# Attention in half blocks: rows of two heads by 64 queries over 192 keys, in a two-layer decoder trunk

## The chip, the core and the metric

The kernel runs on one core of one Trainium2 chip. The time is device microseconds of one execution; for the kernel before, three runs give a median of 1915.66 us (1914.08 to 1919.38). TensorE (PE in the profile, its weight loads PEld), VectorE (DVE), ScalarE (ACT), GpSimd (POOL) and the DMA queues of SyncE (SP) work side by side and wait for each other through semaphores. PSUM, in which matmuls leave their results, is used in banks of 128 x 512 float32.

## The reference

Two layers over 1024 positions of width 1024, float32. In each layer a token mixer (attention on 512 channels beside a causal pooling mixer on the other 512) is followed by a SwiGLU network of width 2816, each between two norms and with a gate. What the change touches is the sliding-window attention: 8 query heads of 64 channels share 2 key heads (4 query heads each), blocks of 128 queries see their own block and the one before, and a query sees the last 128 positions, itself included.

```python
def sliding_window_attention_with_sinks(q, k, v, sinks):
    ...
    k_cat = jnp.concatenate([jnp.pad(kb, pad)[:, :-1], kb], axis=2)
    v_cat = jnp.concatenate([jnp.pad(vb, pad)[:, :-1], vb], axis=2)
    scores = jnp.einsum("bnqkgd,bnskd->bnkgqs", qb, k_cat).astype(jnp.float32)
    scores = scores * (HEAD_DIM ** -0.5)
    ...
    valid = (diff[None] >= 0) & (diff[None] < WINDOW) & (key_abs >= 0)
    scores = jnp.where(valid[None, :, None, None], scores, NEG_INF)
    sink = ...
    probs = jax.nn.softmax(jnp.concatenate([scores, sink], axis=-1), axis=-1)[..., :-1]
    out = jnp.einsum("bnkgqs,bnskd->bnqkgd", probs.astype(v.dtype), v_cat)
    return out.reshape(B, S, N_HEADS * HEAD_DIM)
```

## The kernel before, in words

**Number format.** A float32 value is split into a high part in float32r (a copy on ScalarE, L215) and a low part, what is left (a subtraction on VectorE, L216). A product then takes three matmuls, high by high, high by low and low by high (`mm3`, L254 to L259).

**Stages.** The 1024 positions are worked on in two halves of 512 rows, four token tiles of 128 each. Per layer and half there are projections (`q_pass`, `kv_pass`, `u_pass`), attention, pooling (`pool_mix`), the output projection (`mix_out`), norms, and the SwiGLU network in seven products of half-sized matrices for eight. Each is a generator that yields between pieces; `run` (L640) steps one dense stage and with it the side streams in proportion. The attention of the first half is such a side stream beside the projections of the second half; that of the second half is stepped beside `mix_out` of the first half, then beside `u_pass`, then beside the first products of the SwiGLU network. Two further side streams are the pooling and the sums for the adaptive norm (`ada_sum`, VectorE). A scheduler then orders each engine's instructions over all streams; every engine works through its own list in that order.

**Attention before.** A block is one token tile; a group is one block and one key head n with its four query heads. Per block:

- `att_rotary` (L731) rotates, `att_keys` (L746) splits values and keys. Keys stand as high and low in two orders, are transposed by four matmuls with a unit matrix (L774) and copied twice, as own keys of this block and as earlier keys of the next (`sa`, 256 keys).
- `att_queries` (L790) does the same for four query heads (L798), into `qT`.
- `att_scores` (L806): for each pair u of heads one PSUM bank, two heads of 128 queries by 256 keys, two matmuls each (L813, L814); VectorE adds the mask and takes the row maximum (L816).
- `att_softmax` (L823): exponentials on ScalarE (L835), scaling by the reciprocal sums, three on VectorE (L841) and one on ScalarE (L843).
- `att_probs` (L845): four transposes per pair (L851), then the split into `pth` (ScalarE) and `ph` (VectorE), 512 columns.
- `att_values` (L859): the stationary operand holds the 64 value channels of one key head beside 64 zeros (`vz`), the moving one the transposed probabilities. One three-matmul product each for the earlier and the own keys, 256 columns; everything of a block gathers in one bank `pv`, which one ScalarE copy (L879) takes out.

In `attention` (L885) the scores of a group are written before the probabilities of the group before it, and the values one pair later still. Banks named `msc` come from a ring of three that scores, transposes and the side streams share; `pv` has one bank, `acc`, for the dense stages, four.

## Time and profile before

| | |
|---|---|
| median of 3 runs | 1915.66 us |
| the profiled execution, its own time | 1912.51 us |
| its span, first to last instruction | 1910.7 us |
| granted TensorE clock, mean | 0.997 |
| TensorE busy | 1866.3 us, 98% |
| VectorE busy | 1545.1 us, 81% |
| ScalarE busy | 950.5 us, 50% |
| attention's value matmuls | 384, of 256 columns |
| attention's score matmuls | 256, of 256 columns |
| transposes of probabilities | 256, of 128 columns |

A row such as `L813 PE MATMUL msc<-sa,qT 128*128 128x256` names the line, the engine, what is written and read by the program's tile names, the weights' shape and the result's. A TensorE duration runs from a matmul's start to its modelled end; neighbours overlap, so what one matmul occupies is read from the distance between starts. "Idle before" tells how long an engine stood and for whom.

### The profile page before, as it was taken

Reading aid. Unit: us, or ns where it says so; the run is one execution under the profiler, and the core shown is the slowest. Engines: PE = TensorE matmul, PEld = TensorE weight load, DVE = VectorE, ACT = ScalarE, POOL = GpSimd, SP = SyncE. Lnnn points to the kernel's source line nnn. Section 1 sums busy time; section 2 is a strip of 40 time slices with the busy share of each in tenths; the row PEclk is TensorE's granted clock in tenths of the full one; section 3 lists DMA queues with packets and bytes.
Section 4 is the critical chain, followed back from the end, with each engine's and each line's share of the span. In section 5 each row is a group of like instructions: output and inputs, shape, how many; then the busy total and the mean of one; then the engine's idle time right before and its main releaser. Section 6 shows DMA issues by size and latency. Waiting matters only on the chain.

```text
span 1910.7 us, 26084 instructions
## 1 busy us (share of the span) xinstructions
PE 1866.3 (98%) x8978; PEld 1539.2 (81%) x8978; DVE 1545.1 (81%) x2898; ACT 950.5 (50%) x1789; POOL 26.8 (1%) x84
## 2 busy tenths in 40 slices
PE   6999999999999999999999989999999999999997
PEld 4887788888888888888888868888888887888886
DVE  5999886668898888788879998846889888877687
ACT  4876795653222223445548667845622222244452
POOL 1000000000000000000000000000000000000000
PEclk9999999999999999999999999999999999999999
DMA  9355563555655665944554464536654565574342
GB/s 324 115 155 153 163 226 122 186 177 183 204 179 189 208 207 178 323 137 145 183 168 128 133 183 165 177 110 208 215 188 150 198 209 202 197 252 150 115 152 102
DMA packets 227428, 341.86 MB, mean 179 GB/s; under 512 B 16952, under 2 KB 124360, under 8 KB 227296
## 3 DMA queue, kind: packets, MB, share of 16 engines
q1 hardware_dynamic: 227152, 340.17, 54.2%
q8 instruction: 70, 1.15, 0.2%
q14 instruction: 62, 0.51, 0.1%
q0 software_dynamic: 32, 0.00, 0.0%
q10 hardware_dynamic: 112, 0.04, 0.0%
HBM read 267.25 MB, written 72.89 MB: 178 GB/s over the span
## 4 chain that ended last, share of the span: by engine, by line
PE 79%; DVE 11%; DMA 5%; ACT 3%; issue 1%; SPq 0%; DVEq 0%; ACTq 0%
PE acc L255 24%; PE acc L258 24%; PE acc L259 24%; DMA ar<-in_ada_w_dram 2%; DVE lo L216 2%; DVE ada L289 2%; PE msc L851 1%; PE msc L519 1%; ACT hi L215 1%; DMA raw<-in_w_up_dram 1%; PE pv L255 1%; DVE ph L216 1%; DMA ar<-x 1%; DVE sb L816 1%; PE pv L258 1%
## 5 line engine op out<-in xcount | busy, mean ns | idle before, releaser
L215 ACT ACTIVATE hi<-raw 128x1024 fp32r<-128x1024 f32 (+1 forms) x388 | 332.4, 869 | 365.8 <-PE acc L258 196.2
L216 DVE TENSOR_TENSOR lo<-raw,hi 128x1024 fp32r<-128x1024 f32 (+1 forms) x388 | 380.0, 986 | 123.6 <-ACT hi L215 122.8
L255 PE MATMUL acc<-t,hi 128*128 128x512 f32 x704 | 274.6, 390 | 1.5 <-ACT hi L215 1.5
L258 PE MATMUL acc<-t,hi 128*128 128x512 f32 x704 | 274.0, 389 | 0.0
L259 PE MATMUL acc<-t,lo 128*128 128x512 f32 x704 | 271.9, 389 | 0.0
L255 PE MATMUL acc<-bh,hi 128*128 128x512 f32 x520 | 202.8, 390 | 0.0
L259 PE MATMUL acc<-bh,lo 128*128 128x512 f32 x520 | 202.4, 389 | 0.0
L255 PE MATMUL acc<-hT,hi 128*128 128x512 f32 x480 | 189.7, 395 | 0.6 <-DVE fn L638 0.6
L258 PE MATMUL acc<-hT,hi 128*128 128x512 f32 x480 | 188.4, 392 | 0.0
L259 PE MATMUL acc<-hT,lo 128*128 128x512 f32 x480 | 187.7, 392 | 0.0
L1107 DVE TENSOR_TENSOR fn<-acc,fn 128x512 f32<-128x512 f32 x220 | 150.2, 683 | 37.4 <-PE acc L259 37.4
L255 PEld LDWEIGHTS acc<-t,hi 128*128 128x128 f32 x704 | 132.2, 188 | 30.8 <-ACT hi L215 3.9
L259 PEld LDWEIGHTS acc<-t,lo 128*128 128x128 f32 x704 | 132.2, 188 | 29.0 <-DVE lo L216 1.5
L258 PEld LDWEIGHTS acc<-t,hi 128*128 128x128 f32 x704 | 132.2, 188 | 27.2
L258 PE MATMUL acc<-ph,hi 128*128 128x512 f32 x320 | 124.6, 389 | 0.0
L1043 ACT ACTIVATE fn<-fn 128x512 f32<-128x512 f32 x44 | 27.8, 633 | 180.3 <-DVE fn L1107 180.3
L289 DVE SCALAR_TENSOR_TENSOR ada<-ar,c_act,ada 128x512 f32<-128x512 f32 x140 | 104.6, 747 | 12.0 <-DMA ar<-in_ada_w_dram 11.0
L259 PEld LDWEIGHTS acc<-bh,lo 128*128 128x128 f32 x520 | 97.6, 188 | 20.4
L255 PEld LDWEIGHTS acc<-bh,hi 128*128 128x128 f32 x520 | 97.6, 188 | 20.0
L255 PEld LDWEIGHTS acc<-hT,hi 128*128 128x128 f32 x480 | 90.2, 188 | 18.9 <-DVE fn L638 1.4
L259 PEld LDWEIGHTS acc<-hT,lo 128*128 128x128 f32 x480 | 90.1, 188 | 18.2
L255 PE MATMUL acc<-hi 128*128 128x512 f32 x256 | 101.1, 400 | 2.8 <-DVE fn L638 1.6
(315 smaller groups left out, 3834.6 us busy)
## 6 DMA issues: line engine op xcount, KB each, us to landing
ar<-in_ada_w_dram SPq DMA_DIRECT2D x160, 256.0 KB
raw<-in_w_gate_dram SPq DMA_DIRECT2D x44, 512.0 KB
raw<-in_w_up_dram SPq DMA_DIRECT2D x44, 512.0 KB
raw<-in_w_in_dram SPq DMA_DIRECT2D x80, 256.0 KB
raw<-keeps SPq DMA_DIRECT2D x40, 512.0 KB
keeps<-fn SPq DMA_DIRECT2D x66, 256.0 KB
two_b<-in_w_down_dram SPq DMA_DIRECT2D x30, 512.0 KB
raw<-keepa SPq DMA_DIRECT2D x25, 512.0 KB
```

What stands on the lines that cost most here:

```text
L215: nc.scalar.activation(hi, src, AF.Copy)
L216: recent["split"] = nc.vector.tensor_sub(lo, src, hi.bitcast(F32))
L255: ins = nc.tensor.matmul(dst, lh, rh, start=first, stop=False)
L258: nc.tensor.matmul(dst, lh, rl, start=False, stop=False)
L259: return nc.tensor.matmul(dst, ll, rh, start=False, stop=last)
L289: ins = nc.vector.scalar_tensor_tensor(acc, w, c_act[:, i : i + 1], acc, op0=ALU.mult, op1=ALU.add)
L519: ins = nc.tensor.transpose(bank[:, t * P : (t + 1) * P], src[t], ident)
L816: nc.vector.tensor_tensor_reduce(out=s[:, ii, :], in0=bank[:, ii * 2 * P : (ii + 1) * 2 * P], in1=mask[:, min(blk, 1), :], scale=SCALE, sc ...
L851: nc.tensor.transpose(bank[:, i * P : (i + 1) * P], s[:, ii, ck * P : (ck + 1) * P], ident)
L1043: nc.scalar.activation(g, g, AF.Silu)
L1107: nc.vector.tensor_add(halves_of(dst)[m], bank, halves_of(src)[m])
```

## The change

Rows become half blocks. `att_queries` lays the columns of `qT` out as half (64 queries), head, query, so that a row tile of 128 is two heads by 64 queries of one half. Half h of a block sees the 192 keys from 64 h on (`SPAN`), where all 128 queries saw 256. One mask of 192 columns serves all tiles, and the first block of a layer reads only its own keys (`att_seen`).

A group is now one block and a number r: it holds both halves, half 0 with key head r and half 1 with the other (`n = h ^ r`). A score bank carries 192 + 192 columns. Its 384 columns are transposed as three chunks of 128: half 0's first 128 keys, then a middle chunk whose first 64 columns are half 0's last keys and whose other 64 are half 1's first keys, then half 1's last 128 keys. The outer chunks of both row tiles fill one bank (four transposes, 512 columns to split), the middle chunks another (two, 256 columns).

The value products are three per group for both row tiles together: earlier values of head r, own values of the other head, and for the middle chunk a tile `bd` that holds own values of one head over the first 64 rows beside earlier values of the other head over the last 64. That tile is filled per block by three ScalarE copies (`att_vals`), and `pv` is taken out by four copies over 64 partitions. The value tiles are two, used in turn, and one `bd`, in place of a ring of five; `pth` is one tile of 768 columns in place of two of 512; `qT` has two. Zeros are written once per layer and half of the attention's rooms (`att_room`). Value products of a group are written as one piece, a step before the next group's softmax; the queries of the second key head are written after the first step of a block, and the next block's rotation in the block's second group. In the first block the unseen columns are zeroed on GpSimd.

```diff
-        mix=dict(cfa=2, cfb=2, qkv=6, bqkv=1, uT=4, pt=2, vz=5, rt=1, qT=1, pth=2, pwh=1, pwl=1),
+        mix=dict(cfa=2, cfb=2, qkv=5, bqkv=1, uT=4, pt=2, vz=2, rt=1, qT=2, pth=1, bd=1, pwh=1, pwl=1),
...
+    def att_room():
+        attn["v"] = [t_("vz", [P, 2, 3, HD], F32R) for _ in range(2)]
+        attn["mix"] = t_("bd", [P, 2, 4, HD], F32R)
...
+    def att_vals(blk, qkv):
+        v, mix = attn["v"][blk % 2], attn["mix"]
+        vsrc = qkv[:, QK:QKV].rearrange("p (n d) -> p n d", d=HD)
+        nc.scalar.activation(v[:, 0, 0:3:2, :], vsrc, AF.Copy)
+        nc.vector.tensor_sub(v[:, 1, 0:3:2, :], vsrc, v[:, 0, 0:3:2, :].bitcast(F32))
+        if blk:
+            before = attn["v"][1 - blk % 2]
+            nc.scalar.activation(mix[QH:, :, 0:4:3, :], before[QH:, :, 0:3:2, :].bitcast(F32), AF.Copy)
+        for n in range(NKV):
+            nc.scalar.activation(mix[:QH, :, 2 - n, :], v[:QH, :, 2 * n, :].bitcast(F32), AF.Copy)
...
+    def att_scores(blk, r, u, qTs, mx, s):
         kT = attn["k", blk]
         bank = msc_bank()
-        for ii in range(2):
-            dst = bank[:, ii * 2 * P : (ii + 1) * 2 * P]
-            q = qT[:, (2 * u + ii) * P : (2 * u + ii + 1) * P]
-            nc.tensor.matmul(dst, q, kT[:, 2 * n, :], start=True, stop=False)
-            nc.tensor.matmul(dst, q, kT[:, 2 * n + 1, :], start=False, stop=True)
+        for h in range(2):
+            n, cs = h ^ r, att_seen(blk, h)
+            dst = bank[:, h * SPAN : (h + 1) * SPAN][:, cs]
+            q = qTs[n][:, (2 * h + u) * P : (2 * h + u + 1) * P]
+            for o in range(2):
+                keys = kT[:, 2 * n + o, h * QH : h * QH + SPAN][:, cs]
+                nc.tensor.matmul(dst, q, keys, start=o == 0, stop=o == 1)
...
+    def att_probs(blk, sts, ends, probs):
         bank = msc_bank()
+        chunks = ([0] if blk else []) + [2] if ends else [1]
+        for i in chunks:
+            for u in range(2):
+                at = (i + u) * P
+                nc.tensor.transpose(bank[:, at : at + P], sts[u][:, i * P : (i + 1) * P], ident)
+        cs = slice(chunks[0] * P, (chunks[-1] + 2) * P)
+        to = slice(0, 2 * P) if not ends else slice(chunks[0] * P, 4 * P)
+        split(*(p[:, to] for p in probs), bank[:, cs])
...
+    def att_values(blk, r, probs, pmid, cat, t):
...
+        v, before = attn["v"][blk % 2], attn["v"][1 - blk % 2]
+        at = 2 * (1 - r)
+        parts = [(before, r, probs, 0)] if blk else []
+        parts += [(v, 1 - r, probs, 2 * P), (attn["mix"], at, pmid, 0)]
+        for k, (src, c, (ph, pl), p0) in enumerate(parts):
+            vh, vl = (src[:, j, c : c + 2, :].rearrange("p a d -> p (a d)") for j in range(2))
+            opening, closing = r == 0 and k == 0, r == 1 and k == len(parts) - 1
+            ins = mm3(
+                pv[:, r * 2 * P : (r + 1) * 2 * P], vh, vl, ph[:, p0 : p0 + 2 * P], pl[:, p0 : p0 + 2 * P],
+                opening, closing, None if opening else attn["open"],
+            )
...
+            for n in range(NKV):
+                ns = slice(n * HD, (n + 1) * HD)
+                for h in range(2):
+                    g = h ^ n
+                    nc.scalar.activation(
+                        cat[ns, :, t * P + h * QH : t * P + (h + 1) * QH],
+                        pv[ns, g * 2 * P : (g + 1) * 2 * P].rearrange("p (j q) -> p j q", j=GRP), AF.Copy,
+                    )
...
+            if late:
+                att_values(*late)
+                late = None
+            if cur and r == 1:
+                att_vals(blk, qkvs[t])
```

The change also moves instructions. On TensorE, in the first layer and first half, at the fifth group (the first of the third token tile), its second pair of scores stood among the transposes of the group before it; `sb` holds the probabilities, `sa` the keys. Before:

```order
L258 MATMUL acc<-lo,hT 128x256
L851 MATMUL msc<-ident,sb 128x128
L813 MATMUL msc<-sa,qT 128x256
L851 MATMUL msc<-ident,sb 128x128 x3
L814 MATMUL msc<-sa,qT 128x256
L813 MATMUL msc<-sa,qT 128x256
L814 MATMUL msc<-sa,qT 128x256
L851 MATMUL msc<-ident,sb 128x128 x3
L255 MATMUL pv<-pth,vz 128x256
L851 MATMUL msc<-ident,sb 128x128
L259 MATMUL acc<-hi,hT 128x256
```

and now, with the new line numbers (L836 scores, L883 transposes, L260 to L264 the three-matmul product), the same group:

```order
L264 MATMUL acc<-hi,hT 128x256
L836 MATMUL msc<-sa,qT 128x192 x4
L883 MATMUL msc<-ident,sb 128x128 x4
L836 MATMUL msc<-sa,qT 128x192 x4
L883 MATMUL msc<-ident,sb 128x128 x2
L260 MATMUL acc<-hi,hT 128x256
```

Both pairs of scores and all transposes of the group before now stand in one row of runs, with no dense product between them. The value products of that earlier group follow 24 dense products later, as one piece of nine. Before, a group's value products were two pieces of six, such as this one, behind the first scores of the fifth group:

```order
L813 MATMUL msc<-sa,qT 128x256
L814 MATMUL msc<-sa,qT 128x256
L255 MATMUL pv<-pth,vz 128x256
L258 MATMUL pv<-ph,vz 128x256
L259 MATMUL pv<-pth,vz 128x256
L255 MATMUL pv<-pth,vz 128x256
L258 MATMUL pv<-ph,vz 128x256
L259 MATMUL pv<-pth,vz 128x256
L255 MATMUL acc<-hi,hT 128x256
```

Now:

```order
L264 MATMUL acc<-hi,hT 128x256
L260 MATMUL pv<-pth,vz 128x256
L263 MATMUL pv<-ph,vz 128x256
L264 MATMUL pv<-pth,vz 128x256
L260 MATMUL pv<-pth,vz 128x256
L263 MATMUL pv<-ph,vz 128x256
L264 MATMUL pv<-pth,vz 128x256
L260 MATMUL pv<-pth,bd 128x256
L263 MATMUL pv<-ph,bd 128x256
L264 MATMUL pv<-pth,bd 128x256
L260 MATMUL acc<-hi,hT 128x256
```

On ScalarE, where the third token tile of that half is taken out of `pv` and values are split, before:

```order
L832 ACTIVATE st<-st 128x4
L835 ACTIVATE sb,st<-sb,st 128x256 x4
L879 ACTIVATE cfa<-pv 128x4x128
L755 ACTIVATE vz<-qkv 128x64 x2
L843 ACTIVATE sb<-sb,st 128x256
```

and, at the same place, now (L863 exponentials, L768 values, L774 and L772 the mixed tile, L912 the way out of `pv`):

```order
L858 ACTIVATE st<-st 128x4
L863 ACTIVATE sb,st<-sb,st 128x192
L768 ACTIVATE vz<-qkv 128x2x64
L863 ACTIVATE sb,st<-sb,st 128x192
L774 ACTIVATE bd<-vz 64x2x64
L912 ACTIVATE cfa<-pv 64x4x64 x4
L772 ACTIVATE bd<-vz 64x2x2x64
L774 ACTIVATE bd<-vz 64x2x64
L863 ACTIVATE sb,st<-sb,st 128x192
L220 ACTIVATE hi<-pt 128x512
L870 ACTIVATE sb<-sb,st 128x192
```

The copies into the mixed tile and out of `pv`, which read what value products write or free, now stand among the exponentials of a group, and the last exponential stands behind them.

164 lines of the change are left out of this document (73 added, 91 removed).

## The prediction

> **What bounds the kernel now.** I read the page's busy shares first, then the busy time by stretch, then the order in time on TensorE, then the groups by shape on VectorE and ScalarE.
>
> ```profile
> span 1910.7 us, 26084 instructions
> PE 1866.3 (98%) x8978; PEld 1539.2 (81%) x8978; DVE 1545.1 (81%) x2898; ACT 950.5 (50%) x1789; POOL 26.8 (1%) x84
> ```
>
> TensorE is busy for 98% of the span, so a matmul taken away is time taken away, unless a wait grows in its place. The attention lies in two stretches, one in each layer. The rows give, after the stretch and its length, the busy us of PE, PEld, DVE, ACT and POOL, the granted clock, DMA share and GB/s.
>
> ```profile
> 60.00:260.00 200.00, 194.07 (x1136) 161.38 (x1135) 184.76 (x543) 150.67 (x374) 5.67 (x21) 1.00 0.51 156
> 1000.00:1240.00 240.00, 231.11 (x1332) 193.42 (x1331) 212.67 (x596) 181.04 (x439) 7.18 (x22) 0.99 0.50 157
> 160.00:180.00 20.00, 16.84 (x82) 12.48 (x81) 18.70 (x48) 9.72 (x20) 0.42 (x2) 1.00 0.60 169
> 180.00:200.00 20.00, 18.47 (x95) 14.27 (x95) 19.16 (x48) 13.34 (x34) 0.00 (x0) 1.00 0.69 198
> 260.00:280.00 20.00, 18.80 (x111) 15.89 (x110) 15.53 (x42) 19.70 (x47) 0.27 (x1) 1.00 0.66 209
> 1100.00:1120.00 20.00, 17.26 (x85) 13.38 (x84) 18.60 (x50) 11.85 (x27) 0.00 (x0) 1.00 0.64 182
> 1120.00:1140.00 20.00, 17.25 (x83) 12.72 (x82) 18.44 (x47) 13.29 (x35) 0.00 (x0) 0.95 0.63 183
> 1200.00:1220.00 20.00, 18.80 (x114) 16.05 (x113) 16.84 (x47) 19.71 (x46) 0.27 (x1) 1.00 0.66 214
> ```
>
> In the first stretch TensorE is idle for 6 of 200 us, in the second for 9 of 240, while VectorE is at 92% and 89%: the two are near their limits together. Where TensorE does idle, another engine is full: VectorE at 160 to 200 and 1100 to 1140 (10.2 us of idle TensorE in all), ScalarE at 260 to 280 and 1200 to 1220 (2.4 us). So the change is worth its TensorE time, if VectorE falls with it and ScalarE does not rise too far.
>
> **The change part by part.** A matmul's duration here is its latency; what it occupies is the distance between starts. Columns below: start, length, engine, line, operation, count.
>
> ```profile
> 91.12 0.28 PE L255 MATMUL pv<-pth,vz 128*128 128x256 f32 x1
> 91.24 0.28 PE L258 MATMUL pv<-ph,vz 128*128 128x256 f32 x1
> 91.36 0.28 PE L259 MATMUL pv<-pth,vz 128*128 128x256 f32 x1
> 91.48 0.39 PE L255 MATMUL acc<-hT,hi 128*128 128x512 f32 x1
> 91.71 0.40 PE L258 MATMUL acc<-hT,hi 128*128 128x512 f32 x1
> 158.35 0.93 PE L851 MATMUL msc<-ident,sb 128*128 128x128 f32 x7
> 53.67 0.81 PE L364 MATMUL msc<-ones_r,ar 128*128 128x1 f32 x6
> ...
> 166.06 0.08 PEld L387 LDWEIGHTS msc<-ph,picks 128*4 128x4 f32 x1 [0.95 <-ACT ph L215]
> 166.06 0.19 PEld L255 LDWEIGHTS acc<-hi 128*128 128x128 f32 x1
> ...
> L851 PE MATMUL msc<-ident,sb x256: 270/272/331, 84.2 to 1227.5; 128*128 128x128 f32 x128
> L364 PE MATMUL msc<-ones_r,ar x32: 164/250/266, 23.7 to 54.2; 128*128 128x1 f32 x24, 1*128 1x1 f32 x8
> ```
>
> *Values.* 256 columns occupy 0.12 us (91.12 to 91.48 over three). Per token tile 24 such matmuls become 18, and 12 in the first tile of a layer, which has no tile before it: over 16 tiles 384 become 276. 108 x 0.119 = **12.9 us**.
>
> *Transposes of the probabilities.* A run of seven lasts 0.93 us and one of them 0.27, so they start (0.93 - 0.27) / 6 = 0.11 us apart. The built program issues 184 in place of 256: 72 x 0.11 = **7.9 us**. If one occupied no more than its 128 columns at the slope of the rows above (0.23 us for 512, 0.119 for 256, thus 0.43 ns per column), it would be 0.064 and the term 4.6.
>
> The Trainium skill (TensorE: Matmul & The Clock Gate, Part 4) gives about 275 ns for a transpose in a kernel's context; the median of 272 ns agrees as a latency, but as a price it would make this term 19.8 us, and the run of seven shows that it isn't one.
>
> *Scores.* The same 256 matmuls remain, 224 of them with 192 columns for 256, and 16 each with 128 and 64. By the slope 192 columns need 0.091 us. But six matmuls of a single column start (0.81 - 0.25) / 5 = 0.112 us apart: with almost nothing to stream, something that each matmul brings along lasts 0.11. The load of 128 weight columns is 0.11 longer than that of 4 (0.19 against 0.08), so I take it to be the weight load. Every score matmul loads 128 fresh columns, so I take 0.112, not 0.091: 256 x (0.119 - 0.112) = **1.8 us**. With the slope alone it would be 224 x 0.0275 + 16 x 0.055 + 16 x 0.082 = 8.4.
>
> The Trainium skill speaks on both sides, on the same page: its section LDWEIGHTS has P/1.2 ns for P columns, 107 ns for 128, which the 0.112 bears out; its section Back-to-back issue gap has N/2.4 + 2.5 ns, 82.5 for 192 columns, and by that alone the scores would save 8 us or more.
>
> Sum on TensorE: 12.9 + 7.9 + 1.8 = **22.6 us**, 1.4 per token tile; from 17.5 (4.6 for transposes, nothing for scores) to 29.2 (scores by the slope).
>
> ```profile
> L816 DVE CUSTOM_DVE_ANT_0 sb<-msc,mask 128x256 f32<-128x256 f32 x128 | 50.4, 416 | 6.0 <-PE msc L814 5.6
> L216 DVE TENSOR_TENSOR ph<-msc,pth 128x512 fp32r<-128x512 f32 x64 | 43.7, 686 | 2.6 <-ACT pth L215 2.0
> L841 DVE TENSOR_SCALAR sb<-sb,st 128x256 f32<-128x256 f32 x96 | 28.1, 348 | 0.5
> L287 DVE TENSOR_SCALAR ada<-ar,c_act 128x512 f32<-128x512 f32 x20 | 9.6, 479 | 0.0
> L707 DVE TENSOR_TENSOR qkv<-acc,bqkv 128x512 f32<-128x512 f32 x16 | 10.6, 682 | 0.1
> L696 DVE TENSOR_TENSOR qkv<-acc,bqkv 128x256 f32<-128x256 f32 x12 | 4.4, 413 | 2.6 <-PE acc L259 2.6
> ...
> L835 ACT ACTIVATE sb<-sb,st 128x256 f32<-128x256 f32 x128 | 63.7, 506 | 6.3 <-DVE st L828 6.3
> L215 ACT ACTIVATE hi<-raw 128x512 fp32r<-128x512 f32 x167 | 102.7, 629 | 93.1 <-PE acc L258 35.3 <-PE acc L259 33.3 <-issue 18.6
> L215 ACT ACTIVATE pth<-msc 128x512 fp32r<-128x512 f32 x64 | 37.8, 597 | 22.0 <-PE msc L851 21.8
> L794 ACT ACTIVATE hi<-qkv 128x256 fp32r<-128x256 f32 x32 | 13.2, 412 | 5.7 <-PE acc L259 4.9 <-DVE ada L289 0.8
> L755 ACT ACTIVATE vz<-qkv 128x64 fp32r<-128x64 f32 x32 | 6.6, 252 | 10.9 <-DVE qkv L696 7.4 <-PE pv L259 3.5
> L879 ACT ACTIVATE cfa<-pv 128x512 f32<-128x512 f32 x8 | 4.7, 587 | 0.3 <-PE pv L259 0.3
> L392 ACT ACTIVATE ar<-msc 4x512 f32<-4x512 f32 x2 | 1.2, 588 | 2.0 <-PE msc L388 2.0
> ```
>
> *VectorE.* Two-operand work falls by 1.05 ns per column (682 for 512, 413 for 256), scaling by 0.51 (479, 348). Masks: 53.2 us to 112 x 0.349 + 8 x 0.28 + 8 x 0.215 = 43.0. Probability splits: 64 of 0.686 become 28 of it and 36 of 0.413, 9.7 us less. Scaling: 33.4 to 29.6. Value splits: 32 of 0.23 become 16 of 0.30, 2.7 less. In all 26 us less, 1.6 per tile. TensorE loses 1.4, so neither takes the other's place as the limit.
>
> *ScalarE.* Its slope is 0.85 ns per column (629 for 512, 412 for 256). Exponentials lose 8.2 us, the fourth scaling 2, probability copies 7.8 (28 of 0.597, 36 of 0.38), value copies 3.2. The way out of pv becomes four copies over 64 partitions for one over 128; 4 partitions cost what 128 do (588 against 587), so each of 256 columns costs 0.41: 64 x 0.41 - 16 x 0.587 = 16.8 more. The mixed values are new: 14 of 0.41 and 32 of 0.305, 15.5 more. Together **+11 us**, 0.7 per tile. ScalarE is idle for 49 of the first 200 us, which hides it, but not at 260 to 280 and 1200 to 1220, where it is full: about one tile's 0.7 in each, **+1.5 us** with what queues behind it.
>
> *Waits.* The work between scores and second transposes now stands closer (the order shows four runs, 4 scores, 4 transposes, 4 scores, 2 transposes, back to back in about 12 of 32 groups). All take a bank of a ring of three, so the fourth run needs the first's bank, once VectorE's two mask reductions have read it: 2 x (0.35 + 0.08) = 0.86 us, and half of an instruction in hand, 0.34. TensorE covers 4 x 0.11 + 4 x 0.112 = 0.9 meanwhile. The difference, 0.3 to 0.4 us in 12 groups, is **+5 us**; it could be nothing, since before also has such runs, or 1.2 us each with two splits of 0.69 queued ahead (14). Against it, the 10.2 us that TensorE idles beside a full VectorE hold about three tiles; 3 x 1.6 = **-4.8 us**. Queries of both key heads at a tile's start, the zeroing on GpSimd in a layer's first tile and the four small sink copies have dense products behind them and count as nothing; uncovered, one query chain (0.41 for the high parts, as much for the low, four transposes of 0.11, 0.60 for the copy) is 1.9 us, in 16 tiles 30.
>
> Sum: -22.6 + 1.5 + 5 - 4.8 = **-21 us**. The profiled execution, 1912.5 us, would become 1891.5. It lies 3.2 below the median of the runs, 1915.7; from that I predict **1895 us**, the forecast's own range 1888 to 1902.
>
> **The rivals.**
>
> *Scores shrink with their columns* (for: the slope of the rows; against: the single-column run). 6.6 us more: 1888.
>
> *The fourth run waits longer* (for: VectorE at 92%, so splits queue ahead of the masks; against: the products between runs in the other 20 groups). 14 in place of 5, and VectorE's relief spent in it: -21 + 9 + 4.8 = -7: 1908, or 1903 with the relief kept.
>
> *ScalarE becomes what is waited for*, and the kernel slower. One mixed-value tile, two value tiles and one tile of high probability parts are now reused: the value copies of a token tile must wait until the last value products of the one before have ended, and the exponentials stand behind them in ScalarE's queue. The row of such a wait before:
>
> ```profile
> ACT vz L755 <- PE pv L259: 1.7, 1, 1.7
> ```
>
> At 1.7 us and 0.7 of added work in every tile, 16 x 2.4 = 38 us against 22.6: +16, 1931. It decides from 1.4 us per tile on the path. For it speaks the order on ScalarE, where the copies stand ahead of the tile's last exponential; against it the quarter of ScalarE's time that is idle, and the 24 products of TensorE after the value products, which do not wait for these exponentials.
>
> *The change removes no work on TensorE* is excluded by the counts of the built program (184, 276, narrower scores).
>
> **How the numbers follow.** Forecast 0.60; narrow scores 0.12; longer fourth run 0.18; ScalarE 0.10. What this kernel's measurement tells from no change is about 0.3%, 5.7 us: faster is below 1910, slower above 1921. The first two are faster throughout, of the third 0.13, of the last 0.01 (partly hidden): 0.86. Same: 0.05 of the third and 0.03 of the last, 0.08. Slower: 0.06. The range 1880 to 1910 takes in the first two, their bounds (29.2 on TensorE and all relief kept) and most of the third, and leaves out ScalarE's case.
>
> **What would show it.** Right: 276 value matmuls 0.12 us apart; 192-column scores about 0.112 apart, not 0.09; VectorE's busy time about 26 us lower, ScalarE's about 11 higher; TensorE's idle time in both stretches within 5 us of before. Wrong: waits of the transposes for the masks above 10 us in total, or ScalarE's waits for the value products above 1 us per tile with TensorE idle behind the probability copies.

## The result, and the profile after

The changed kernel takes 1931.0 us (median of 6 runs, 1924.2 to 1939.2), the kernel before 1914.6 (6 runs, 1913.0 to 1919.4): a ratio of 1.0086, 95% interval 1.0060 to 1.0112, so 16.5 us or 0.9% slower. Forecast were 1895 us, 1880 to 1910. The profiled execution took 1924.2 us, the shortest of the six and 11.7 more than that of before; the readings below are about these 11.7.

The first lines of the page of the changed kernel, and its two attention stretches by engine (busy us of PE, PEld, DVE, ACT and POOL, granted clock, DMA share, GB/s):

```profile
span 1922.4 us, 25765 instructions
PE 1851.3 (96%) x8798; PEld 1522.8 (79%) x8798; DVE 1523.7 (79%) x2888; ACT 956.1 (50%) x1867; POOL 15.9 (1%) x65
...
60.00:260.00 200.00, 183.05 (x1030) 150.85 (x1029) 172.16 (x520) 147.71 (x393) 2.45 (x10) 0.98 0.48 151
1000.00:1240.00 240.00, 217.91 (x1225) 180.81 (x1225) 193.61 (x587) 177.91 (x465) 3.80 (x19) 0.97 0.49 152
```

TensorE idles 17 and 22 us in stretches where it idled 6 and 9 before, VectorE's share falls from 92% and 89% to 86% and 81%, and the clock is lower. Three groups on TensorE take most of the new waits: the transposes of the probabilities, the transposes of the normalised rows, and the products of a side stream that sums the conditioning weights (names `picks`). Of the kernel before, then of the changed one; behind the bar stand busy us, mean ns, and the idle us ahead of the group with what ended it:

```profile
L851 PE MATMUL msc<-ident,sb 128*128 128x128 f32 x256 | 43.7, 277 | 4.0 <-DVE sb L841 3.0 <-ACT raw L512 0.6 <-DVE st L816 0.3
L519 PE MATMUL msc<-ident,fn 128*128 128x128 f32 x192 | 28.1, 276 | 0.1
L387 PE MATMUL msc<-ph,picks 128*4 128x512 f32 x8 | 3.2, 395 | 0.5 <-ACT ph L215 0.5
```

```profile
L883 PE MATMUL msc<-ident,sb 128*128 128x128 f32 x184 | 36.2, 293 | 17.1 <-DVE sb L868 11.8 <-DVE st L839 2.2 <-ACT raw L517 1.7
L524 PE MATMUL msc<-ident,fn 128*128 128x128 f32 x192 | 28.1, 277 | 5.1 <-DVE fn L506 2.8 <-DVE ph L221 1.4 <-ACT fn L508 0.8
L392 PE MATMUL msc<-ph,picks 128*4 128x512 f32 x8 | 3.2, 394 | 5.5 <-ACT ph L220 5.5
```

Only the first group belongs to the attention; the other two are as many as before and only wait longer for VectorE and ScalarE.

**An account of TensorE.** From the starts of all matmuls in a trace, TensorE's time can be split. Each matmul *streams* for as long as starts lie apart where nothing waits (0.228 us for 512 columns, 0.118 for 256, 0.112 for scores of 192 and fewer, 0.109 for transposes of probabilities, 0.084 for those of keys and queries); what then passes until the next start is *lost*. I count losses from 60 us on, and apart those that fall into stretches at half clock (below).

| kernel | streams | lost, full clock | lost, half clock | stretches at half clock |
|---|---|---|---|---|
| before | 1840.2 | 58.1 | 1.6 | 1 |
| changed | 1818.0 | 85.3 | 9.5 | 6 |

TensorE streams 22.2 us less: the forecast's 22.6 is there. It loses 35.1 more, 27.2 at full clock and 7.9 at half. That is the whole difference between the two traces; the question is why the losses grow. By the same account the three groups above (with all products of `picks`) lose about 13 us before and 42 now, which covers all of the growth at full clock. Only half of it, some 15 us, lies in the attention's own transposes.

**The half clock.** Rows of the changed kernel, three windows of 3.41 us one behind the other, and of the kernel before its only such place:

```profile
143.39:146.80 3.41, 0.76 (x4) 0.29 (x2) 2.71 (x12) 3.37 (x11) 0.00 (x0) 1.00 0.08 32
146.80:150.22 3.42, 3.37 (x10) 2.80 (x11) 2.88 (x6) 1.73 (x4) 0.00 (x0) 0.50 0.16 32
150.22:153.63 3.41, 3.41 (x23) 3.07 (x23) 3.41 (x12) 1.89 (x5) 0.00 (x0) 1.00 0.55 162
```

```profile
1134.59:1138.00 3.41, 1.81 (x4) 0.57 (x4) 3.41 (x7) 1.45 (x3) 0.00 (x0) 0.99 0.46 151
1138.00:1141.41 3.41, 3.31 (x8) 2.63 (x9) 3.25 (x11) 2.28 (x9) 0.00 (x0) 0.51 0.54 156
```

Each time a window in which TensorE is busy for only part of the time (0.76 and 1.81 of 3.41 us) is followed by one at half clock. The section on the hardware has this over all traces.

### The profile page after: what moved, and what is told of

The parts are those of the page before. It is cut to its first block, busy times and chain, and to the rows that moved or that the text cites. A ratio compares the mean times of both kernels' runs of the same rounds, so it can differ in the third digit from the quotient of the medians.

```text
span 1922.4 us, 25765 instructions
## 1 busy us (share of the span) xinstructions
PE 1851.3 (96%) x8798; PEld 1522.8 (79%) x8798; DVE 1523.7 (79%) x2888; ACT 956.1 (50%) x1867; POOL 15.9 (1%) x65
## 4 chain that ended last, share of the span: by engine, by line
PE 74%; DVE 11%; ACT 7%; DMA 6%; issue 2%; SPq 0%; DVEq 0%; ACTq 0%
PE acc L260 23%; PE acc L263 23%; PE acc L264 23%; DMA ar<-in_ada_w_dram 3%; DVE lo L221 2%; DMA raw<-in_w_up_dram 2%; DVE ada L294 2%; ACT hi L220 1%; ACT sb L863 1%; PE msc L524 1%; DVE ph L221 1%; ACT junk L481 1%; PE msc L883 1%; DVE sb L868 1%; DVE fn L1146 1%
## 5 line engine op out<-in xcount | busy, mean ns | idle before, releaser
L260 PE MATMUL acc<-t,hi 128*128 128x512 f32 x704 | 274.6, 390 | 1.6 <-ACT hi L220 1.6
L264 PE MATMUL acc<-t,lo 128*128 128x512 f32 x704 | 271.8, 389 | 0.0
L260 PE MATMUL acc<-bh,hi 128*128 128x512 f32 x520 | 202.7, 390 | 0.0
L264 PE MATMUL acc<-bh,lo 128*128 128x512 f32 x520 | 202.4, 389 | 0.0
L260 PE MATMUL acc<-hT,hi 128*128 128x512 f32 x480 | 191.2, 398 | 1.9 <-DVE fn L643 1.0
L264 PE MATMUL acc<-hT,lo 128*128 128x512 f32 x480 | 188.5, 393 | 0.0
L260 PEld LDWEIGHTS acc<-t,hi 128*128 128x128 f32 x704 | 132.1, 188 | 31.0 <-ACT hi L220 4.1
L264 PEld LDWEIGHTS acc<-t,lo 128*128 128x128 f32 x704 | 132.1, 188 | 29.0 <-DVE lo L221 1.4
L264 PEld LDWEIGHTS acc<-bh,lo 128*128 128x128 f32 x520 | 97.6, 188 | 20.4
L260 PEld LDWEIGHTS acc<-bh,hi 128*128 128x128 f32 x520 | 97.6, 188 | 20.2
L260 PEld LDWEIGHTS acc<-hT,hi 128*128 128x128 f32 x480 | 90.3, 188 | 20.4 <-DVE fn L643 2.2
L264 PEld LDWEIGHTS acc<-hT,lo 128*128 128x128 f32 x480 | 90.5, 189 | 18.7 <-issue 0.2
L263 PEld LDWEIGHTS acc<-hT,hi 128*128 128x128 f32 x480 | 90.5, 189 | 16.9
```

Of the source, the lines that this page charges most:

```text
L260: ins = nc.tensor.matmul(dst, lh, rh, start=first, stop=False)
L263: nc.tensor.matmul(dst, lh, rl, start=False, stop=False)
L264: return nc.tensor.matmul(dst, ll, rh, start=False, stop=last)
```

## The experiments

Theories stood against each other in groups. On the change's own parts: **A**, the copies of values on ScalarE stand among the exponentials; **B**, the fourth run of a group waits for VectorE's masks and a bank; **C**, the new order makes large pieces. Then, as these fell: **D**, the softmax of all four row tiles must end before the first transposes; **E**, the engines are so close to their limits together that TensorE's time becomes idle time; **F**, the length of one group's chain decides; **Q** and **R**, a shortened ring of tiles; **U**, the uneven split over the two groups of a token tile. The kernel before ran along each time, at 1912.9 to 1915.1 us; ratios are to it, with 95% intervals.

**1. The copies of values (A).** The place that suggested A, in the order of time in the changed kernel (start, length, engine, line, operation, count, idle time before it):

```profile
141.24 0.46 ACT L863 ACTIVATE sb<-sb,st 128x192 f32<-128x192 f32 x1 [2.07 <-DVE st L854]
...
142.04 0.44 ACT L863 ACTIVATE sb<-sb,st 128x192 f32<-128x192 f32 x1
...
142.48 0.29 ACT L768 ACTIVATE vz<-qkv 128x128 fp32r<-128x128 f32 x1
...
142.68 0.44 ACT L863 ACTIVATE sb<-sb,st 128x192 f32<-128x192 f32 x1
...
143.34 0.31 ACT L774 ACTIVATE bd<-vz 64x128 fp32r<-64x128 f32 x1
...
143.56 1.29 ACT L912 ACTIVATE cfa<-pv 64x256 f32<-64x256 f32 x4
...
144.86 0.41 ACT L772 ACTIVATE bd<-vz 64x256 fp32r<-64x256 f32 x1
...
145.29 0.31 ACT L774 ACTIVATE bd<-vz 64x128 fp32r<-64x128 f32 x1
...
145.50 0.44 ACT L863 ACTIVATE sb<-sb,st 128x192 f32<-128x192 f32 x1
...
146.07 0.16 DVE L864 TENSOR_TENSOR st<-st 128x4 f32<-128x4 f32 x1 [0.56 <-ACT sb L863]
...
146.48 0.78 DVE L868 TENSOR_SCALAR sb<-sb,st 128x192 f32<-128x192 f32 x3
...
146.85 0.48 PE L883 MATMUL msc<-ident,sb 128*128 128x128 f32 x1 [2.70 <-DVE sb L868]
```

Three exponentials run from 141.24 to 143.1, with one copy among them; then seven more copies come, and the fourth starts at 145.50. The sum waits for it, the scalings for the sum, the transposes for the scalings, and TensorE stands still for 2.70 us. Over all 32 groups the run of four exponentials lasts 3.31 us on the mean, with 102 instructions that aren't the softmax's between them (2.25 us and 6 before, although each exponential was longer then). Three runs take this apart: the mixed-value copies on GpSimd; no such copies and one copy out of the value bank; the softmax written ahead of the values.

```
e1_bd_pool
-            nc.scalar.activation(mix[QH:, :, 0:4:3, :], before[QH:, :, 0:3:2, :].bitcast(F32), AF.Copy)
+            for j in range(2):
+                nc.gpsimd.tensor_copy(mix[QH:, j, 0:4:3, :], before[QH:, j, 0:3:2, :].bitcast(F32))
-            nc.scalar.activation(mix[:QH, :, 2 - n, :], v[:QH, :, 2 * n, :].bitcast(F32), AF.Copy)
+            nc.gpsimd.tensor_copy(mix[:QH, :, 2 - n, :], v[:QH, :, 2 * n, :].bitcast(F32))
e2_no_copies: both lines above replaced by pass, and four copies out of pv by
+            nc.scalar.activation(cat[:, :, t * P : (t + 1) * P], pv.rearrange(...), AF.Copy)
e3_softmax_first: in attention()
+            if prev:
+                att_softmax(pblk, pr, sts, mx, nsink)
             if late:
                 att_values(*late)
```

> The change with its three copies into the mixed tile moved from ScalarE to GpSimd (the earlier values as two copies of 64 partitions x 128 columns). Theory A, value copies on ScalarE stand among the exponentials of a group, the last exponential is late, the transposes wait and TensorE idles: ScalarE's busy time falls by about 15 us (956 to 941), TensorE's wait of the transposes for the scaling falls from 11.8 to about 6 us, and the time from 1931 to about 1920. Theory C, the new order makes large pieces (nine value products, runs of scores and transposes side by side) and TensorE finds nothing ready between them, whoever copies: the time moves by less than 4 us. Theory B, the fourth run waits for VectorE's masks on the ring of three banks: no change in time, and the wait for the masks stays near 2 us.

> The change without the three copies into the mixed tile, and with one copy out of pv over 128 partitions and 512 columns in place of four (the middle chunk's values are left zero and half of the attention's output lands in the wrong columns; all other work is the same). An upper bound on the copies. Theory A: ScalarE falls by about 30 us, the transposes' waits go back to the 3 us of before, the clock's half-rate stretches vanish, and the time is about 1900, below the kernel before. Theory C: not below 1920.

> The change with the softmax of a group written ahead of the value products and value copies of the group before it, the same instructions in all. Theory A: the exponentials stand together on ScalarE, the transposes' wait for the scaling falls below 5 us and the time to about 1915. Theory C: within 4 us of the change, since the pieces stay as large.

Measured: e1 1931.3 us (1.0089, 1.0070 to 1.0109), e2 1927.0 (1.0080, 1.0063 to 1.0096) and e3 1928.1 (1.0078, 1.0059 to 1.0097). With ScalarE busy for 24 us less (e2), 4 of the 16.5 us come back by the medians and 1 by the ratios; with the exponentials closer together again (2.42 us on the mean in e3), 3 and 1.5. None of this is clear of the intervals. A is not the main cause. The third run shows why, at the same place of the program:

```profile
143.92 0.44 ACT L863 ACTIVATE sb<-sb,st 128x192 f32<-128x192 f32 x1
...
144.15 0.69 DVE L991 SCALAR_TENSOR_TENSOR pt<-pt,uT 128x512 f32<-128x512 f32 x1
144.76 0.15 DVE L864 TENSOR_TENSOR st<-st 128x4 f32<-128x4 f32 x1
...
145.17 0.70 DVE L987 TENSOR_TENSOR pt<-uT 128x527 f32<-128x527 f32 x1
145.79 0.77 DVE L868 TENSOR_SCALAR sb<-sb,st 128x192 f32<-128x192 f32 x3
...
146.16 0.33 PE L883 MATMUL msc<-ident,sb 128*128 128x128 f32 x1 [2.42 <-DVE sb L868]
```

The last exponential now ends 1.6 us earlier, at 144.4. But VectorE has pooling sums in its queue ahead of the scalings, and TensorE still waits 2.42 us. The wait has only changed its engine.

**2. Large pieces and banks (C, B).** The value products in two pieces, between scores and transposes of each half step, with the value copies behind (and a tile of its own for the middle part).

```
e4_pieces
+                if late:
+                    att_values(*late, u)
                 if prev:
-                    att_probs(pblk, sts, u == 0, (probs, pmid)[u])
+                    att_probs(pblk, sts, u == 0, new[u])
```

> The change with the value products of a group in two pieces (six and three), each written between the scores and the transposes of a half step as the kernel before does, with the value copies behind them; the same matmuls and copies. Theory C: the transposes' waits go back to about 5 us and the time to 1900 to 1908. Theory A: as the run with the softmax first, about 1915, since the exponentials stand ahead of the copies here too; with the copies' 11 us of ScalarE left, not below 1910.

Measured: 1927.9 us (1.0076, 1.0061 to 1.0091), which neither theory had. C falls. B had fallen with the profile after: the transposes wait 2.2 us in all for the masks (`DVE st L839` above).

**3. The softmax chain (D, F).** The softmax a step earlier; the front part first, which needs only two row tiles; no scaling at all; the transposes a step later.

```
e5_softmax_early: att_softmax(prev) moved ahead of the group's first yield
e6_front_first
-        chunks = ([0] if blk else []) + [2] if ends else [1]
+        chunks = ([0] if blk else []) if front else [1, 2]
e12_no_scaling: the loop that scales the four row tiles left out of att_softmax
e13_later_transposes: att_probs(ends) behind att_scores(u = 1), att_probs(middle) in the next
  group's first step, att_values behind that group's att_scores(u = 0)
```

> The changed kernel with the softmax of a group written one attention step earlier: in the step that writes the next group's keys and queries, and not in the step behind it that writes the values. Nothing is added or left out. Theory D (the softmax of all four row tiles must now be over before the group's first transposes, where two row tiles were enough before, so the chain of four exponentials and four scalings ends too late for TensorE): the waits of the transposes of probabilities for the scalings of VectorE nearly vanish, TensorE's idle time in the two attention stretches falls by 10 to 15 us, time 1914 to 1920. Theory E (VectorE or ScalarE sets the pace in these stretches, so that a saving on TensorE only becomes idle time there): the waits move to other places, time 1926 to 1934.

> The changed kernel with the key parts transposed in another grouping: the first half step of a group takes only the front part, which needs only the first two of the four row tiles, and the second half step the middle and the back part together, which need all four. The layout of the probability tiles follows; nothing is added or left out. Theory D: the slack that the kernel before had is back without moving the softmax, the waits of the transposes for the scalings fall to about half, time 1916 to 1923. Theory E: 1926 to 1934.

> The changed kernel with the scaling of the four row tiles by the reciprocal of their sums left out (so the output is wrong): three VectorE instructions of 0.315 us and one of ScalarE of 0.454 a group, 30 us of VectorE and 14 of ScalarE in all, and the transposes need only the exponentials. Theory F: each group's chain is 0.9 to 1.4 us shorter, about what TensorE's cover lost, so most of the new waits vanish, time 1900 to 1912. Theory E: it helps as far as VectorE has less to do, half as much as taking away 60 us of the sums: 1912 to 1922.

> The changed kernel with the transposes of the probabilities one attention step later: the front and back parts of a group behind the second half of the next group's scores (in the changed kernel behind the first half), the middle part at the start of the group after it, the value products one step later too. Nothing is added or left out. Counted in the traces, TensorE has 9.89 us of work between a group's last score product and its first transpose in the kernel before and 8.51 in the changed kernel (0.75 of the loss are dense products that now stand on the other side of the transposes), and idles 1.09 and 1.88 us there, in each of 32 groups. Theory F (this cover decides: masks, exponentials and scalings take about 10 to 11 us from the scores to the transposes whatever TensorE does): with about 2 us more cover the waits of the transposes vanish, TensorE's idle time falls by 20 us or more, time 1905 to 1915. Theory E (VectorE sets the pace): the idle time moves to other places, time 1924 to 1934.

Measured: e5 1937.6 us (1.0123, 1.0108 to 1.0138), slower than either theory had it, e6 1930.5 (1.0085, 1.0068 to 1.0102), e12 1923.1 (1.0045, 1.0027 to 1.0064) and e13 1929.5 (1.0079, 1.0055 to 1.0103). Each of the four does shorten the waits of the transposes; by the account they fall from 24.7 us to 15.6, 17.2, 13.5 and 14.6. And each time others grow. In the last run these groups stand where the changed kernel has 17.1, 1.2, nothing and nothing:

```profile
L883 PE MATMUL msc<-ident,sb 128*128 128x128 f32 x184 | 31.3, 281 | 10.0 <-DVE sb L868 2.4 <-ACT raw L517 2.3 <-ACT cfa L984 1.9
L836 PE MATMUL msc<-sa,qT 128*128 128x192 f32 x224 | 37.6, 284 | 6.5 <-DVE st L839 5.3 <-ACT qT L814 1.3
L809 PE MATMUL msc<-ident,hi 128*128 128x128 f32 x128 | 15.9, 248 | 4.2 <-ACT sa L798 4.2
L260 PE MATMUL msc<-hi,pwh 128*128 128x512 f32 x16 | 7.1, 445 | 3.5 <-DVE st L839 3.5
```

TensorE has 10.9 us of work between a group's last scores and its first transposes there, more than the 9.9 of the kernel before, and still idles 2.6 us in it (1.1 in the kernel before, 1.9 in the changed one). D falls with the second run, F with the last. Leaving out the scaling gives 8 us, for 44 us less on VectorE and ScalarE.

**4. What an engine's time is worth (E).** A known amount of TensorE's work was taken from the kernel before and added to the changed one; VectorE's was taken from both.

```
e7_more_products: 4 times in att_values
+                    more = nc.tensor.matmul(pv[:HD, ...], v[:, 0, 1, :], ph[:, p0 : p0 + 2 * P], start=False, stop=False)
e8_before_fewer: in att_values of the kernel before, the third product of mm3 (vl, ph) left out
e9_less_vector, e10_before_less_vector: in ada_sum
             for i, w in enumerate(ws, j - 2):
+                if i % 2:
+                    continue
```

> The changed kernel with TensorE work put back: four further products a group, of zero weights (64 columns) with 256 columns of the probabilities, into the value bank. They add nothing to the output. 32 groups x 4 x 0.119 = 15.2 us of TensorE's time. Theory E (another engine sets the pace): TensorE's new idle time takes them up, time 1928 to 1936, so within 5 us of the changed kernel. Theory D: the waits for the softmax lie at the transposes and the products at another place, so most of them are paid, time 1941 to 1947.

> The kernel before with TensorE work taken away and nothing else: the products of the values' low parts with the probabilities' high parts are left out (so the output is a little less exact), 8 of 24 in each of 16 token tiles, 128 x 0.119 = 15.2 us. Theory E: the time taken from TensorE turns into idle time in the kernel before as well, time 1908 to 1914. Theory D (the loss comes from the changed kernel's own order of softmax and transposes): the kernel before turns nearly all of it into time, 1897 to 1902.

> The changed kernel with VectorE work taken away that has nothing to do with attention: in the side stream that sums the rows of the conditioning weights, every second row is left out of the sum (so the output is wrong; the loads, the splits and the products remain). That is 80 instructions of 0.747 us, 60 us of VectorE, about 36 of them in the two attention stretches. Theory E (VectorE sets the pace there, and the time taken from TensorE has become idle time): TensorE's idle time above its cadence falls by 20 us or more and the time to 1900 to 1912. Theory F (the length of one group's chain of masks, exponentials, scalings and transposes decides, not how full VectorE is; TensorE has 8.9 us of work between a group's last scores and its first transposes, 10.3 in the kernel before): the chain stays as long as it is, time 1922 to 1932.

> The kernel before with the same half of those sums left out. Theory E: VectorE sets the pace in the kernel before too, only less; time 1900 to 1908. Theory F: TensorE's work covers the chains there, time within 3 us of the kernel before, 1911 to 1917.

| run | edit | time | ratio, interval | streams | lost, full clock | lost, half clock |
|---|---|---|---|---|---|---|
| before, 15.2 us less on TensorE | e8 | 1910.9 | 0.9981, 0.9972 to 0.9991 | 1825.1 | 65.1 | 10.2 |
| before, 60 us less on VectorE | e10 | 1899.3 | 0.9919, 0.9900 to 0.9938 | 1840.2 | 44.8 | 1.5 |
| changed, 60 us less on VectorE | e9 | 1916.8 | 1.0010, 0.9998 to 1.0021 | 1818.0 | 80.0 | 6.2 |
| changed, 15.2 us more on TensorE | e7 | 1950.5 | 1.0186, 1.0162 to 1.0210 | 1833.1 | 89.7 | 16.2 |

The first row matters most for the prediction. In the kernel before, with nothing else changed, 15.2 us less of TensorE's work, all of it value products, bring 3.75 us (1.7 to 5.4): a quarter. Its profile's first line, to be held against 98% and 1866.3 before:

```profile
PE 1859.3 (97%) x8850; PEld 1529.5 (80%) x8850; DVE 1541.9 (81%) x2898; ACT 950.8 (50%) x1789; POOL 31.1 (2%) x84
```

By the account the time went to half the clock (8.6 us, five stretches where there was one) and to waits (7.0); this trace is of the second slowest of ten executions, 2.8 us above the median, so it shows that much too large a loss. VectorE's time is worth as much in both kernels: 60 us bring 15.7 and 14.2. Here are the attention stretches of the kernel before with that relief:

```profile
60.00:260.00 200.00, 197.81 (x1173) 167.35 (x1172) 173.42 (x530) 156.49 (x392) 5.28 (x21) 1.00 0.51 162
1000.00:1240.00 240.00, 234.58 (x1346) 198.33 (x1345) 200.45 (x558) 183.77 (x441) 5.92 (x22) 0.99 0.51 163
```

TensorE is at 99% and 98%, so part of what it lost was lost to VectorE (58.1 us at full clock became 44.8). What comes back in the changed kernel lies at another place. First the kernel before with that relief (e10), then the changed one (e9):

```profile
L853 PE MATMUL msc<-ident,sb 128*128 128x128 f32 x256 | 43.3, 276 | 1.6 <-DVE sb L843 0.9 <-ACT raw L514 0.6
L885 PE MATMUL msc<-ident,sb 128*128 128x128 f32 x184 | 34.7, 286 | 15.7 <-DVE sb L870 9.4 <-DVE st L841 2.9 <-ACT raw L519 1.9
L394 PE MATMUL msc<-ph,picks 128*4 128x512 f32 x8 | 3.2, 397 | 0.0
```

In the kernel before the waits of the probabilities' transposes fall from 4.0 us to 1.6. In the changed one they stay, 15.7 for 17.1, while those of the `picks` products vanish (5.5 to nothing; by the account, with all products of `picks`, 9.7 to 0.3). The half sums shorten the very stream that feeds these products, so e9 doesn't show that VectorE's load makes the new waits of the attention.

E doesn't explain the whole. If both rates held for the work that the change takes away, and added up, the change, with 22 us less on TensorE and 21 on VectorE, should have come out some 11 us faster (an estimate, 22 x 0.25 + 21 x 0.26). And e7 speaks against E: adding to TensorE in the changed kernel costs all of it and more (19.5 for 15.2, outside the ranges of both theories), where an engine with 39 idle us might have taken it up. e9 fell between the ranges of its two theories.

**5. Rings and queries (Q, R, U).** What the change had to give up for room, and the last uneven thing in its order.

```
e14_before_qkv5           - qkv=6   + qkv=5     (kernel before)
e15_before_pth1           - pth=2   + pth=1     (kernel before)
e16_no_copies_qkv6        - qkv=5   + qkv=6     (changed, no bd tile, one copy out of pv)
e17_no_copies_pth2        - pth=1   + pth=2     (the same)
e18_queries_ahead
                 if r == 0:
-                    qTs.append(att_queries(1, qkvs[t]))
+                    qTs.append(att_queries(1, qkvs[t]) if t == 0 else ahead)
+                elif t + 1 < NT:
+                    ahead = att_queries(1, qkvs[t + 1])
```

> The kernel before with one number changed: five tiles for the queries, keys and values in place of six, as in the changed kernel. Nothing is added or left out. Theory Q (the dense products of the next half's queries, keys and values write into these tiles; with five, they must wait until the attention is through with one token tile more, so the dense work that covers the chains is held back): a loss of 10 to 20 us, 1924 to 1935. Theory R (the single tile of high probability parts holds the chains back) and theory E (the coupling of the engines, whatever the rings): within 3 us of the kernel before, 1911 to 1918.

> The kernel before with one number changed: one tile for the high parts of the probabilities in place of two, as in the changed kernel (there it is half as long again and holds a whole group; here the splits of a half step must wait for the value products of the half step before). Theory R: a loss of 10 us or more, 1925 or above. Theories Q and E: within 5 us of the kernel before, up to 1920.

> The changed kernel with six tiles for queries, keys and values, as in the kernel before. For the room, the tile of mixed values is gone: its copies are left out, the middle parts are multiplied with the unmixed values, and the way out of the value bank is one copy of 128 x 512 (so the output is wrong); buffers that stood at 576 columns have 528. With five tiles this form took 1926.95 us. Theory Q: the time falls to 1905 to 1915. Theories R and E: 1922 to 1931.

> The same form (no tile of mixed values, unmixed values in its place, one copy out of the value bank, so the output is wrong) with five tiles for queries, keys and values and two tiles for the high parts of the probabilities. Theory R: the time falls to 1905 to 1918. Theories Q and E: 1922 to 1931.

> The changed kernel with the queries of the second key head of a token tile made ahead, in the second group of the tile before it, in place of at the tile's own start; only a layer half's first tile still makes both at its start. A third tile of transposed queries makes the room for that, and buffers that stood at 576 columns have 528. Nothing is added or left out. Theory U (both queries at the tile's start load the first group with 0.4 us of transposes and the chain of copies behind them, and leave TensorE short of work in the second): the first group falls from 14.8 to about 13.5 us, the second stays at about 12.4, TensorE's idle time falls by 12 us or more, time 1910 to 1918. Theory E (the engines wait for each other in turn, and the idle time keeps its sum wherever the work is written): 1924 to 1934.

Measured: e14 1912.9 us (0.9995, 0.9986 to 1.0004), e15 1917.5 (1.0014, 1.0003 to 1.0024), e16 1928.5 (1.0083, 1.0064 to 1.0103), e17 1929.0 (1.0081, 1.0062 to 1.0100) and e18 1932.3 (1.0094, 1.0075 to 1.0112). Q, R and U fall; one tile for the high parts costs the kernel before 0.1%, and a second one gives the changed kernel nothing.

**6. Work that VectorE can hand over.** If VectorE's time is what the attention lacks, the kernel before should gain when GpSimd, idle for 99% of the span, takes the rotary and the pooling windows.

```
e20_before_gpsimd (kernel before)
-        nc.vector.tensor_mul(tmp[:, 0], t1, cb)          and the five that follow
+        nc.gpsimd.tensor_mul(tmp[:, 0], t1, cb)
-                nc.vector.tensor_add(nxt[:, lo:n], cur[:, lo:n], cur[:, lo - width : n - width])
+                nc.gpsimd.tensor_add(nxt[:, lo:n], cur[:, lo:n], cur[:, lo - width : n - width])
```

> The kernel before with two pieces of VectorE work written for GpSimd: the six rotary instructions of each token tile (96 of 0.234 us) and the running sums of the pooling windows (40 of 0.70 us). Nothing is added or left out; VectorE has 50.5 us less to do, all of it in or beside the attention stretches. Theory E (VectorE's load sets the pace there): at the 0.26 us per us that the half sums gave, 13 us less, 1897 to 1906, and faster than both kernels. Rival: GpSimd takes longer over the same work (its 128x64 casts took 0.30 us, VectorE's 128x80 products 0.23) and what waits for the windows and the rotary comes late, or its reads slow VectorE; no gain or a loss, 1911 to 1930.

Measured: 1921.5 us (1.0037, 1.0028 to 1.0046), so slower. The page, and a small VectorE group:

```profile
PE 1866.4 (97%) x8978; PEld 1538.9 (80%) x8978; DVE 1528.7 (80%) x2762; ACT 950.1 (50%) x1789; POOL 125.6 (7%) x220
...
L947 POOL TENSOR_TENSOR pt<-uT 128x527 f32<-128x527 f32 x16 | 20.3, 1269 | 60.2 <-issue 40.2 <-DVE pt L956 11.6 <-DVE pt L951 6.6
...
L831 DVE TENSOR_TENSOR st<-st,sk 128x4 f32<-128x4 f32 x32 | 7.0, 218 | 0.3
```

GpSimd takes 1.27 us for what VectorE does in 0.70. 50.5 us of instructions left VectorE, but those that stayed took 22 us longer in sum (in the row above 218 ns, 156 in the kernel before), and its busy time, in which overlapping instructions count once, fell by only 16.4. The rival of that expectation holds; which of its two halves weighs more, the run doesn't tell. No version that does all the work beats the kernel before by more than the intervals.

## Why the prediction was wrong

The sum on TensorE was right, term by term. 276 value products lie 0.120 us apart (median in the trace, 0.12 forecast) and 184 transposes 0.110 (0.11). Scores of 192 columns lie 0.113 us apart, and those of 64 columns 0.112: what a matmul brings along sets them, not their columns, so the rival of narrow scores is out. Streaming fell by 22.2 us for 22.6.

The terms on the other engines were right too: masks 9.9 us less (10.2 forecast), splits 9.6 (9.7), scaling 3.7 (3.8), values 2.9 (2.7); on ScalarE the mixed values cost 15.5 (15.5) and the way out of pv 14.3 more (16.8). The page has VectorE 21 us lower for 26 and ScalarE 6 higher for 11. In sum of durations VectorE is 23 lower: four small sink copies per layer and slightly longer other instructions take back 3.

**The step that failed** is the first, "So the change is worth its TensorE time, if VectorE falls with it and ScalarE does not rise too far", and with it the term "Waits" (+5 and -4.8), which stands at +35. TensorE's 98% was read as the limit; e8 and e10 show that it was one of two: value products taken from the kernel before return a quarter of their time, and VectorE's relief returns time with TensorE's work as it was. The 92% of VectorE in the same rows, quoted there, hinted at it; I took it as a condition and not as the price. The relief of 4.8 had the right cause but was a credit beside the full TensorE sum, where by the rates of experiment 4 it was about half of what there was to get (5.5 of 11).

The forecast of the fourth run named the wrong partner. The transposes do wait, not for the masks' bank (2.2 us), but for the scalings (11.8). "Queries of both key heads ... count as nothing" held (e18). Of the signs that I had named, the one for idle time failed (within 5 us of before; it is 24 more in the two stretches), while neither sign of a cause appeared: the mask waits stayed under 10 us, and ScalarE waited 4.5 us in all for value products (3.2 for the value tiles, 1.3 on the way out of pv).

The rival that gave 1931 us, with ScalarE waited for, met the number, and the picture in experiment 1 is its picture. But without all of those copies the time stays at 1927, so the mechanism holds for some 4 of 16.5 us at most. The number is a coincidence.

**What is open.** Shown are where the time goes (35 us lost on TensorE, 7.9 of them at half clock), that value products taken from the kernel before return only a quarter of their time, and that VectorE's load has a share in that kernel's waits. For the changed kernel that share isn't shown, since what e9's trace gains at full clock lies with `picks`. Not shown either is what the changed order costs beyond that, by estimate about 27 us (16.5 measured, 11 of gain expected by the rates of experiment 4). Ten versions of the changed kernel with copies, softmax, products, transposes, rings or queries placed otherwise took 1927 to 1938 us, and lost 85 to 94 us at full clock against 85.3. The sum of the waits stayed while their place changed. That speaks against any single one of these parts, and for in-order queues of three engines with much to do in this stretch (after the change TensorE 92% and 91%, VectorE 86% and 81%, ScalarE 74% in both), so that any of them passes the wait on. The rows of experiment 1 show this once; that it is so for the whole sum is my reading, and no run proved it.

## What to carry to other kernels

A busy share of 98% does not make an engine's time the price of a change when another engine stands at 92% beside it: take a known amount of work off the one engine with nothing else changed, and see what share comes back (a quarter, here) and at which waits. Count what a change does to the chains through in-order engines, and not only to their sums, since copies put between the exponentials of a group can make every engine behind them late. And once such waits are there, taking one out may only move it to the next queue, so judge a repair by the sum of the waits and not by the one it aimed at.

## What the runs showed of the hardware

**Half clock without an idle stretch of 3.4 us.** In 19 of the 20 traces the granted clock fell to 0.5 somewhere beyond the first 30 us and before the end, in 85 places in all, always for 3.41 us or twice that, and within a trace all of them start on one grid of 3.413 us. What stands before them is a grid window in which TensorE lost, in pieces, about 2 us. Lost is meant as in the account above; the profile's own idle time, which counts a matmul as busy to its modelled end, is smaller (1.60 us in the row of the kernel before). Of 75 to 80 windows at full clock with 2.05 us lost or more (the count moves with 0.1 us in where a window is taken to start), 72 or 73 were followed by half clock, and of all windows under 1.9 us only 2 to 4. No single long gap is needed: the longest was 0.9 us before one such place of the kernel without copies. Each stretch at half clock costs TensorE 1.6 us, waits in it included (9.5 us over 20.5 in the changed kernel). The Trainium skill (TensorE: Matmul & The Clock Gate, Part 1) has the free-running window of 3413 ns, which these starts bear out; it lets the clock fall after an idle window, and these traces show that three fifths of one are enough. By these figures idle time on TensorE has a step in its price: 2 us of waits that fall into one window cost 1.6 us more than the same waits apart.

**What a matmul brings along.** Scores of 64 columns start 112 ns apart and of 192 columns 113 (medians), with 128 fresh weight columns each. From 192 columns to 64 the narrower moving side saved nothing.

**GpSimd beside VectorE.** 99 us of added GpSimd work made VectorE's own instructions longer by about 22 us in sum; four-column ones went from 156 to 218 ns.
